# Key norms spread by TensorE, x sums in row groups, angles ahead of the products, and a statistics sum kept on chip, in a gated convolution and dilated attention block on one core

## The chip, the cores and the metric

The kernel runs on one core of one Trainium2 chip. A core has five engines that work beside each other: TensorE (PE) for products, VectorE (DVE), ScalarE (ACT) and GpSimd (POOL) for elementwise work, and SyncE (SP), which here issues the DMAs (transfers). Data lie in on-chip memory of 128 partitions (SBUF), products arrive in eight accumulator banks of 128 x 512 numbers (PSUM), and what doesn't fit goes to the memory off chip (DRAM, names that end in `_d`). Each engine works through its own queue and waits for the others by semaphores. The metric is the device time of one execution in microseconds (us).

## What is computed

One decoder layer on x of 2048 tokens by 1024 channels, all in float32:

```python
mod = silu(c) @ w_ada + b_ada
shift, scale, gate = split(mod, 3)
h = rms_norm(x, norm_w) * (1 + scale) + shift
a, b, g_conv, q, k, v, g_attn, m_conv, m_attn = split(h @ w_in, SPLIT_POINTS)

u = depthwise_causal_conv(a * sigmoid(b), conv_w, conv_b)     # 31 taps
u = silu(layer_norm(u, conv_ln_w, conv_ln_b)) * silu(g_conv)
y_conv = u @ w_conv_out

q = rope(rms_norm(q, q_norm_w), positions)                    # 12 heads of 128
k = rope(rms_norm(k, k_norm_w), positions)
# three groups of four heads; query t attends t, t-d, ..., t-window
# (window, dilation) = (128, 1), (512, 4), (2048, 16)
o = sum over groups of softmax(lse)[g] * attention(q, k, v)[g]
y_attn = (o * silu(g_attn)) @ w_attn_out

out = (sigmoid(m_conv) * y_conv + sigmoid(m_attn) * y_attn) @ w_out
x = x + gate * out
```

Three sums of this matter below: the mean square of each token of x, the mean square of each head of the keys (a "K-norm", one per token and head), and the mean over channels that `layer_norm` takes of the convolution's output.

## The kernel before, in words

The tokens are worked in two halves of 1024. The large product with `w_in` is done by a scheme with seven products instead of eight for each 2 x 2 block of quarters (A11, A12, A21, A22 of the activations, B11 to B22 of the weights, with sums such as S1 and T1), each with its numbers split in a high and a low part, so that one quarter product is twelve matmuls of 128 x 512 (lines 310 to 314). Such a group of twelve is a **product** here; there are 562. ACT makes the high parts, DVE or POOL the low ones, and POOL or ACT and DVE the sums. The first sixteen products of half 0 use plain quarters (`PLAIN`, line 304), because the sums of quarters are not there yet.

The program numbers the products (slots) and keeps an agenda: `at_slot(s, f, where)` (line 470) puts a piece of other work beside product s, at a place in it ("act", "vec", "tail", "store" and so on). PE's queue and, in most of the kernel, those of DVE, ACT, POOL and SP follow the order in which the program issues the work; an instruction that waits holds up those behind it in its engine's queue.

The stages, in order: the start (loads of x and w_ada, the squares of x, their mean, the scaling by the adaLN numbers `mod`; the rope's sines and cosines, called angles, made on DVE in two big tiles), half 0's queries, keys and values with the attention of its heads, half 0's gates and convolution, the same for half 1, the end of the convolution, then the layer norm and the output projections in blocks.

Places that the change touches:

- *K-norms* (`rotate`, lines 579 to 704, called once for each of 12 pairs of query heads and 12 of key heads; `which` is 0 for queries, 1 for keys). ACT squares the projected heads; PE sums the squares over channels into a few rows of a bank (`sums`, line 602), ACT copies these out (`rows`). For queries PE turns the rows by two transposes (`queries`, line 613), DVE adds epsilon, POOL takes the power -1/2 (`query_roots`, line 621). For keys the rows go to DRAM in four stores and come back by a load into `stk`, one token in each partition (`keys`); POOL makes the roots (`key_roots`); these go to DRAM (`rsk_d`) and come back by two loads that repeat them over 64 partitions each into `rsk` (`key_spread`); DVE multiplies both tiles of the heads by it (`key_scale`, line 644, two instructions of 128 x 1024).
- *turn_v* (line 564): values are transposed on PE into bank "t" (line 570), copied by ACT to `vev` (line 572) and stored.
- *Banks* (line 80): tags z, s and o have two banks each, t and u one each.
- *The squares of x*: `x_square` (line 881) squares one 128 x 512 tile on ACT and sums over channels on PE with the squares as the stationary operand, four products with one output column each; `x_roots` (line 888) adds epsilon and takes the root; `x_spread` (line 894) has PE spread the four columns of roots over 128 x 512; `x_scale` (line 900) multiplies. `first_part` (line 928) makes the high and low part of an A quarter, the low part on the engine that it is given.
- *later_x* (lines 1204 to 1222): half 1's tokens are loaded in rows, squared with a sum on ACT; the roots of 1024 tokens are stored to `rsx_d` and come back spread.
- *Weight sums* T1 to T4 of half 0's first columns are made on POOL (`sum_weights`) and stored for half 1.
- *The statistics sum*: `usum` is the sum over channel blocks of the convolution's output; each half's is stored to `usum_d`, and after the convolution the whole is loaded into a tile of 128 x 2048 (line 1446). PE sums it over partitions into `pm` (line 1498), from which the layer norm `d` goes on. The projections' input `ma` is loaded behind (line 1584), and DVE makes `yt` of it and the product `ya` (line 1590).

## Time and profile before

| | |
|---|---|
| median of 3 runs | 2518.55 us (2515.42 to 2518.6) |
| profiled execution, its time | 2517.68 us |
| its span in the profile | 2515.7 us |
| mean granted clock of PE | 0.965 |
| DMA | 463.39 MB, mean 184 GB/s |

A span is what lies between the first and the last instruction of the profiled execution. A row of a timeline has the start, the length, the engine, the line of the kernel, the operation, what it writes and reads, and in brackets how long the engine was idle before and for what it waited. A row of the stages gives, for a stretch of time, the busy time of PE, PE's weight loads, DVE, ACT, POOL (with the number of instructions each), the granted clock of PE, the share of the DMA engines and GB/s.

### The profile page before, as it was taken

To read this page: it belongs to the slowest core of one execution; us is meant where nothing else is said; L and a number is where in the kernel's file an instruction comes from. 1 tells how busy PE (TensorE), PEld (TensorE's weight loads), DVE (VectorE), ACT (ScalarE), POOL (GpSimd) and SP (SyncE) were. 2 spreads that over 40 slices of the span, in tenths; PEclk is the share of its full clock that TensorE was granted. 3 is DMA by queue.
4 is the path that set the end of the run, shared out by engine and by line. 5 is a ranking of instruction groups with operands and counts; after the bars stand their busy time and mean duration, and the time that the engine had idled before them with its cause. 6 is when DMAs were issued, how large, how long until landed. Compare 5 with 4: busy or idle time off the path is not lost. (4 is left out here: it accounts for less than half of the span.)

```text
span 2515.7 us, 34990 instructions
## 1 busy us (share of the span) xinstructions
PE 2347.1 (93%) x11628; PEld 1903.8 (76%) x11628; DVE 1763.4 (70%) x2889; ACT 1072.5 (43%) x2163; POOL 1100.2 (44%) x860
## 2 busy tenths in 40 slices
PE   7879789999989999989799899999999988999999
PEld 6556567777878888767688778787888866888887
DVE  5768674762699999955654454558999977877644
ACT  3643344444554444534444334553444443422311
POOL 2466444435445779825433233445656640000231
PEclk8889989999999999989999999999999998999999
DMA  7465567557654446643666555755445458876553
GB/s 257 151 167 173 150 224 217 162 185 241 203 183 159 150 151 197 209 153 108 174 178 197 173 163 181 248 170 170 158 133 155 143 187 307 290 262 200 176 160 104
DMA packets 313116, 463.39 MB, mean 184 GB/s; under 512 B 34468, under 2 KB 138212, under 8 KB 312808
## 3 DMA queue, kind: packets, MB, share of 16 engines
q1 hardware_dynamic: 298664, 435.46, 55.4%
q10 hardware_dynamic: 14272, 25.72, 2.8%
q8 instruction: 91, 1.49, 0.2%
q14 instruction: 89, 0.73, 0.1%
HBM read 293.99 MB, written 167.06 MB: 183 GB/s over the span
## 5 line engine op out<-in xcount | busy, mean ns | idle before, releaser
L247 POOL TENSOR_TENSOR slT<-wT,shT 128x512 fp32r<-128x512 f32 x192 | 259.6, 1354 | 283.7 <-ACT shT L246 253.4
L247 POOL TENSOR_TENSOR slB<-wB,shB 128x512 fp32r<-128x512 f32 x142 | 190.5, 1342 | 194.5 <-ACT shB L246 172.1
L246 ACT ACTIVATE shB<-wB 128x512 fp32r<-128x512 f32 x234 | 147.3, 630 | 201.6 <-issue 38.0
L247 POOL TENSOR_TENSOR slT<-wB,shT 128x512 fp32r<-128x512 f32 x94 | 126.8, 1353 | 174.7 <-ACT shT L246 148.9
L246 ACT ACTIVATE shT<-wT 128x512 fp32r<-128x512 f32 x198 | 124.2, 628 | 170.6 <-DMA wT<-tT_d 27.7
L372 DVE SCALAR_TENSOR_TENSOR ce<-ut,chan,ce 128x512 f32<-128x512 f32 x240 | 179.8, 749 | 3.6
L401 DVE SCALAR_TENSOR_TENSOR ce<-us,pair_taps,ce 128x512 f32<-128x512 f32 x240 | 179.8, 749 | 3.2
L385 DVE SCALAR_TENSOR_TENSOR cq<-ut,chan,cq 128x512 f32<-128x512 f32 x208 | 154.9, 745 | 0.0
L778 DVE CUSTOM_DVE_ANT_0 sm<-ps,mask,rqq 128x256 f32<-128x256 f32 (+1 forms) x192 | 78.1, 444 | 102.5 <-PE ps L766 73.8
L241 POOL TENSOR_TENSOR wB<-wB,wB 128x512 f32<-128x512 f32 x76 | 105.5, 1388 | 57.2 <-DVE slB L247 38.7
L246 ACT ACTIVATE shT<-wB 128x512 fp32r<-128x512 f32 x114 | 71.5, 628 | 83.0 <-PE paab L314 24.9
L796 DVE COPY pT<-ptp 128x512 f32<-128x512 f32 (+2 forms) x96 | 58.8, 612 | 55.2 <-PE ptp L794 54.9
L247 DVE TENSOR_TENSOR slB<-wB,shB 128x512 fp32r<-128x512 f32 x92 | 70.8, 771 | 37.8 <-ACT shB L246 19.0
L819 PE MATMUL po<-v,pT 128*128 128x128 f32 x560 | 84.8, 283 | 11.7 <-DVE pT L796 11.7
L819 PEld LDWEIGHTS po<-v,pT 128*128 128x128 f32 x560 | 77.1, 196 | 19.5 <-DVE pT L796 12.2
L137 POOL TENSOR_SCALAR stf<-stf 128x4 f32<-128x4 f32 x4 | 1.4, 340 | 200.7 <-DVE stf L1514 142.1
L766 PE MATMUL ps<-qk 128*128 128x128 f32 x512 | 79.0, 284 | 0.0
L1686 ACT ACTIVATE yh<-yq 128x512 fp32r<-128x512 f32 x48 | 27.3, 623 | 117.8 <-POOL yq L1680 46.1
L766 PEld LDWEIGHTS ps<-qk 128*128 128x128 f32 x512 | 69.8, 201 | 0.3 <-issue 0.2
L785 ACT ACTIVATE sm<-sm,osb 128x256 f32<-128x256 f32 (+1 forms) x128 | 58.3, 458 | 13.3 <-DVE osb L778 9.7
L825 ACT ACTIVATE osb<-po 128x256 f32<-128x256 f32 x64 | 24.7, 386 | 87.9 <-PE po L819 87.3
L644 DVE TENSOR_TENSOR spare_lo<-spare_lo,rsk 128x1024 f32<-128x1024 f32 x16 | 20.8, 1302 | 58.8 <-DMA rsk<-rsk_d 58.8
(798 smaller groups left out, 7832.5 us busy)
## 6 DMA issues: line engine op xcount, KB each, us to landing
wB<-in_w_in_dram SPq DMA_DIRECT2D x272, 256.0 KB
wT<-tT_d SPq DMA_DIRECT2D x160, 256.0 KB
tT_d<-wB SPq DMA_DIRECT2D x114, 256.0 KB
qk<-qk_d SPq DMA_DIRECT2D x96, 256.0 KB
v_d<-vev SPq DMA_DIRECT2D x48, 256.0 KB
qk_d<-spare_hi SPq DMA_DIRECT2D x48, 256.0 KB
qk_d<-spare_lo SPq DMA_DIRECT2D x48, 256.0 KB
v<-v_d SPq DMA_DIRECT2D x96, 128.0 KB
```

Of the source, the lines that this page charges most:

```text
L241: nc.gpsimd.tensor_tensor(dst, x0, x1, op=ALU.subtract)
L246: nc.scalar.activation(h, q[name], AF.Copy)
L247: eng.tensor_tensor(l, q[name], h.bitcast(F32), op=ALU.subtract)
L372: stt(box["e"], e[:, 1 + j : 513 + j], chan[:, cb, 2 * j : 2 * j + 1], box["e"], op0=ALU.mult, op1=ALU.add)
L385: stt(box["o"], o[:, 2 + j : 514 + j], w, psum_o, op0=ALU.mult, op1=ALU.add)
L401: stt(dst, box["both"][:, 1 + j : 513 + j], pair_taps[:, cb, j : j + 1], box["e"], op0=ALU.mult, op1=ALU.subtract if j == 0 else ALU.add)
L766: nc.tensor.matmul(ps[:, c : c + P], box["q"][i], kt, start=True, stop=True)
L778: nc.vector.tensor_tensor_reduce(sm[:, a:z], ps[:, a:z], m[:, 256 - (z - a) :], rq[:, b, u % 2 : u % 2 + 1], 3e38, ALU.add, ALU.min, box[" ...
L785: nc.scalar.activation(sm[:, a:z], sm[:, a:z], AF.Exp, scale=-1.0, bias=box["low"][i], accum_out=box["total"][i])
L796: nc.vector.tensor_copy(valid(pT), valid(pt))
L819: nc.tensor.matmul(po[:, P * i : P * i + P], box["pT"][:, c : c + P], vt, start=(m == 0), stop=(m == count[i] - 1))
L1686: nc.scalar.activation(h, src, AF.Copy)
```

## The change

**Keys.** The two transposes, DVE's epsilon (`more`) and POOL's root (`roots`) now serve queries and keys alike. For keys PE then spreads the roots: `spread(c)` is eight products with a column of roots, repeated 64 times, as the stationary operand and the identity as the moving one, which fill one bank; DVE scales two half tiles of 128 x 512 from that bank, and the second `spread` uses the same bank "t" after that. The four stores, the load, the store and the two repeating loads are gone. The squares' sums, the rows and the transposes stand one product earlier; the first spread stands two products behind the transposes, the second one more. `turn_v` uses banks t and u in turn.

**The start.** Squares of x are summed with a 32-wide block of ones as the stationary operand and the squares as the moving one, in four row groups, into 128 columns; DVE copies the rows, and PE transposes them. For the second half of the columns x's scaling takes in adaLN's scale. All low parts of these first quarters are made on DVE, all low parts of the plain weights on POOL. The order of `PLAIN` changes (ten splits instead of twelve), and the second part of w_ada is loaded ahead of B21 and B22. Of the angles' steps nine stand ahead of x's roots and eight more ahead of x's scaling, instead of six ahead and the rest beside the first products. The permuted copies of the angle tables go from ACT to POOL.

**Other places.** `later_x` moves from slots 7 to 15 to slots 21 to 38, and its roots are spread by PE (two times four products, copied by ACT) and not through `rsx_d`. The weight sums of half 0's first columns are no longer made and stored; half 1 makes them itself. Half 0's `usum` is stored and loaded back when half 1's convolution opens, into one half of the wide tile; half 1's sum is made in the other half of it, so that no store and load stand ahead of `pm`.

The core of the diff:

```diff
-            if cb == KC - 1:
-                nc.sync.dma_start(usum_d[:, HS * half : HS * half + HS], us)
+            if cb == KC - 1 and half == 0:
+                nc.sync.dma_start(usum_d, us)
...
-                pt = bank("t", f"pt{n}_{col}{c}")
+                pt = bank("tu"[i % 2], f"pt{n}_{col}{c}")
...
+        def turned():
+            pt = box["pt"] = bank("t", f"prq{n}")
             for c in range(2):
                 nc.tensor.transpose(pt[:, P * c : P * c + P], box["rows"][:, c], ident)
-            st = box["st"] = rb["p"].tile([P, 48], F32, tag="st", name=f"st{n}", bufs=1)
-            got = pt[:, : 2 * P].rearrange("p (c q m) -> p c q m", c=2, q=4)[..., :2]
+
+        def more():
+            st = box["st"] = rb["p"].tile([P, 32], F32, tag="st", name=f"st{n}", bufs=2)
+            got = box["pt"][:, : 2 * P].rearrange("p (c q m) -> p c q m", c=2, q=4)[..., :2]
             nc.vector.tensor_scalar(st[:, :16].rearrange("p (c q m) -> p c q m", c=2, q=4), got, EPS, None, op0=ALU.add)
 
-        def query_roots():
+        def roots():
             st = box["st"]
-            rq = edge.tile([P, 16], F32, tag="rq", name=f"rq{n}", bufs=4)
             nc.gpsimd.tensor_tensor(st[:, 16:32], st[:, :16], mhalf, op=ALU.pow)
-            nc.gpsimd.tensor_scalar(rq, st[:, 16:32], ISQ, None, op0=ALU.mult)
-            heads_rq[half, u0] = rq.rearrange("p (b m) -> p b m", m=2)
-
-        def keys():
-            ss = dram.tile([2, HS], F32, name=f"ss{n}_d")
-            for q in range(4):
-                nc.sync.dma_start(ss.rearrange("h (c q i) -> q h c i", c=2, q=4)[q], box["rows"][32 * q : 32 * q + 2])
-            st = box["st"] = rb["p"].tile([P, 48], F32, tag="st", name=f"st{n}", bufs=1)
-            nc.sync.dma_start(st[:, :16], ss.rearrange("h (p c) -> (h p) c", c=16))
-
-        def key_roots():
-            st = box["st"]
-            rsqrt_cols(st[:, 32:48], st[:, :16], 16, st[:, 16:32])
-
-        def key_spread():
-            rs_d = dram.tile([2, HS], F32, name=f"rs{n}_d")
-            nc.sync.dma_start(rs_d.rearrange("h (p c) -> (h p) c", c=16), box["st"][:, 32:48])
-            rs = box["rs"] = rp["p"].tile([P, HS], F32, tag="rs", name=f"rs{n}", bufs=1)
-            for h in range(2):
-                nc.sync.dma_start(rs[64 * h : 64 * h + 64], rs_d[h][None, :].to_broadcast([64, HS]))
-
-        def key_scale(i):
-            return lambda: tt(reg[i], reg[i], box["rs"], op=ALU.mult)
+            if which == 0:
+                rq = edge.tile([P, 16], F32, tag="rq", name=f"rq{n}", bufs=4)
+                nc.gpsimd.tensor_scalar(rq, st[:, 16:32], ISQ, None, op0=ALU.mult)
+                heads_rq[half, u0] = rq.rearrange("p (b m) -> p b m", m=2)
+
+        def spread(c):
+            def f():
+                rs = box["rs"] = bank("t", f"rs{n}_{c}")
+                for q in range(4):
+                    for m in range(2):
+                        a = 16 + 8 * c + 2 * q + m
+                        nc.tensor.matmul(rs[64 * m : 64 * m + 64, P * q : P * q + P], box["st"][:, a : a + 1].to_broadcast([P, 64]), ident,
+                                         start=True, stop=True, skip_group_check=True)
+            return f
+
+        def key_scale(c, i):
+            x = reg[i][:, 512 * c : 512 * c + 512]
+            return lambda: tt(x, x, box["rs"], op=ALU.mult)
...
-            start, last = e6 + 2, e6 + 4
+            start, last = e6 + 2, e6 + 3
             count = (3, 3, 3, 3) if which else (3, 3, 2, 2, 2)
         else:
-            sq = ((e4 + 1, 0, 0), (e5, 1, 1), (e5 + 1, 0, 1), (e6 + 1, 1, 0))
-            start, last = e5 + 2, e6 + 3
-            count = (3, 3, 2, 2, 2) if which else (2,) * 6
+            sq = ((e4, 0, 0), (e4 + 1, 1, 1), (e6, 0, 1), (e6 + 1, 1, 0))
+            start, last = e6, e6 + 2
+            count = (2,) * 6
         for s, c, i in sq:
-            at_slot(s, square(c, i), "act2")
-            at_slot(s + 1, sums(c, i), "tail")
+            at_slot(s, square(c, i), "act" if s > e6 else "act2")
+            at_slot(max(s, e6 - 2), sums(c, i), "tail")
...
-        at_slot(last, rows, "act2")
+        at_slot(last, rows, "act")
+        at_slot(last, turned, "tail")
+        at_slot(last + 1, more)
+        at_slot(last + 1, roots)
         if which == 0:
-            at_slot(last + 1, queries, "tail")
-            at_slot(last + 2, query_roots)
             for i in range(2):
                 at_slot(end, store(i), "load")
         else:
-            at_slot(last, keys, "store")
-            at_slot(last + 1, key_roots)
-            at_slot(last + 2, key_spread, "store")
-            s = last + 3
-            assert s >= end
+            for c in range(2):
+                at_slot(last + 2 + c, spread(c), "tail")
+                for i in range(2):
+                    at_slot(last + 3 + c, key_scale(c, i))
+            assert last + 3 + 1 >= end - 1
             for i in range(2):
-                at_slot(s + i, key_scale(i))
-                at_slot(s + i + 1, store(i), "load")
-            kept_by[half, u0] = s + 2
+                at_slot(last + 5, store(i), "load")
...
+    def x_sum(k, t, pm):
+        sq = squares.pop((k, t))
         for b in range(4):
-            nc.tensor.matmul(pm[:, b : b + 1], sq[:, P * b : P * b + P], ones[:, :1],
-                             start=(k == 0 and b == 0), stop=(k == KC - 1), skip_group_check=True)
-
-    def x_roots(t, pm):
-        st = su.tile([P, 12], F32, tag="xst", name=f"xst{t}", bufs=2)
-        nc.vector.tensor_scalar(st[:, 8:12], pm[:, :4], EPS, None, op0=ALU.add)
+            nc.tensor.matmul(pm[32 * b : 32 * b + 32, :P], ones[:, :32], sq[:, P * b : P * b + P],
+                             start=(k == 0), stop=(k == KC - 1), skip_group_check=True)
+
+    def x_rows(t, pm):
+        rows = su.tile([P, 512], F32, tag="sq", name=f"xrow{t}", bufs=5)[:, :P]
...
+    def x_roots(t, pm, rows):
+        nc.tensor.transpose(pm[:, P : 2 * P], rows, ident)
...
+    angle_steps(9)
     pm = bank("t", "xm0")
     for k in range(KC):
-        x_square(k, 0, pm)
-    pr = x_spread(0, x_roots(0, pm))
-    for k in range(KC):
-        x_scale(k, 0, pr)
+        x_square(k, 0)
+        x_sum(k, 0, pm)
+    st = x_roots(0, pm, x_rows(0, pm))
+    angle_steps(8)
...
+    def later_spread(c):
+        pr = bank("o", f"rsx{c}")
+        for b in range(4):
+            a = 24 + 4 * c + b
+            nc.tensor.matmul(pr[:, P * b : P * b + P], xst1[:, a : a + 1].to_broadcast([P, P]), ident, start=True, stop=True)
+        nc.scalar.activation(xh["rs"][:, 512 * c : 512 * c + 512], pr, AF.Copy)
...
+        if half:
+            sums_of["p"] = ctx.enter_context(pool("sum"))
+            wide = sums_of["u"] = sums_of["p"].tile([P, S], F32, tag="wide", name="usum")
+            nc.sync.dma_start(wide[:, :HS], usum_d)
         p = opened(cv, pool("cv"))
-        cv["usum"] = p.tile([P, HS], F32, name=f"usum{half}")
+        cv["usum"] = wide[:, HS:] if half else p.tile([P, HS], F32, name="usum0")
...
-    sp = ctx.enter_context(pool("sum"))
-    usum = sp.tile([P, S], F32, tag="wide", name="usum")
-    nc.sync.dma_start(usum, usum_d)
+    sp, usum = sums_of["p"], sums_of["u"]
```

How the order moves on the engines, at three places. First, DVE at the second key pair of half 1. `spare_lo` holds the keys that are scaled, `rsk` the roots, `sm` and `osb` the scores of a head's attention, `pT` a transposed attention tile. Before:

```order
L778 ISA sm_1_3_11211,osb_1_3_11210<-ps_1_3_11205,mask,rqq_0_10486 128x256
L778 ISA osb_1_3_11210 128x1
L778 ISA sm_1_3_11211,osb_1_3_11210<-ps_1_3_11205,mask,rqq_0_10486 128x256
L778 ISA osb_1_3_11210 128x1
L644 TENSOR_TENSOR spare_lo<-spare_lo,rsk_1_11200 128x1024
L512 TENSOR_TENSOR spare_hi<-spare_hi,pcq_2_11089 128x32x16
L796 COPY pT_1_2_11237<-ptp_1_2_11232 128x512
L644 TENSOR_TENSOR spare_lo<-spare_lo,rsk_1_11200 128x1024
```

After:

```order
L657 TENSOR_TENSOR spare_lo<-spare_lo 128x512
L658 TENSOR_TENSOR spare_lo<-tmk_1_10_11144,tmk_1_11_11146 128x512
L635 TENSOR_TENSOR spare_lo<-spare_lo,rsk_1_0_11205 128x512 x2
L768 ISA sm_1_3_11283,osb_1_3_11282<-ps_1_3_11277,mask,rqq_0_10494 128x256
L768 ISA osb_1_3_11282 128x1
L768 ISA sm_1_3_11283,osb_1_3_11282<-ps_1_3_11277,mask,rqq_0_10494 128x256
L768 ISA osb_1_3_11282 128x1
L635 TENSOR_TENSOR spare_lo<-spare_lo,rsk_1_1_11256 128x512 x2
L507 TENSOR_TENSOR spare_hi<-spare_hi,pcq_2_11155 128x32x16
L786 COPY pT_1_2_11310<-ptp_1_2_11305 128x512
```

The scaling of the first columns now stands ahead of the scores and that of the second columns behind them, where the first scaling of 128 x 1024 stood; no scaling stands behind the copy `pT` any more. On PE, the two spreads of this pair stand at the end of one product and of the next (`paq` and `pak` are the banks of products, `ptp` an attention tile's transposes); the first of them with its surroundings:

```order
L309 MATMUL paq_2_10962<-S_hi_9810,shT_1_4096_11069 128x512
L309 MATMUL paq_2_10962<-S_lo_9811,shT_1_4096_11069 128x512
L309 MATMUL paq_2_10962<-S_hi_9810,slT_1_4096_11070 128x512
L629 MATMUL rsk_1_0_11205<-ident,stk_1_11148 64x128 x8
L784 MATMUL ptp_1_1_11214<-ident,sm_1_1_11101 128x128 x4
L309 MATMUL pak_2_11241<-A_hi_9526,shB_1_5632_11106 128x512
L309 MATMUL pak_2_11241<-A_lo_9527,shB_1_5632_11106 128x512
L309 MATMUL pak_2_11241<-A_hi_9526,slB_1_5632_11107 128x512
```

There was nothing between `paq` and `ptp` before; what is behind the spread in this queue goes on only when the roots `stk` are there.

Second, DVE at the start. `spare_lo` and `spare_hi` are the angles, `xm` the sums of squares, `xst` the four columns for the roots, `xr` their spread, `hf` the tiles of x. Before:

```order
L944 TENSOR_SCALAR spare_lo<-spare_lo 128x1024
L890 TENSOR_SCALAR xst_307<-xm_258 128x4
L901 TENSOR_TENSOR hf_0_171<-hf_0_171,xr_310 128x512
L901 TENSOR_TENSOR hf_0_172<-hf_0_172,xr_310 128x512
L901 TENSOR_TENSOR hf_0_173<-hf_0_173,xr_310 128x512
```

After:

```order
L952 TENSOR_TENSOR spare_hi<-spare_hi,spare_lo 128x1024
L955 SCALAR_TENSOR_TENSOR spare_hi<-spare_lo,spare_hi 128x1024
L955 SCALAR_TENSOR_TENSOR spare_hi<-spare_hi 128x1024
L885 COPY xrow_309<-xm_260 128x128
L891 TENSOR_SCALAR xst_312<-xm_260 128x4
L955 SCALAR_TENSOR_TENSOR spare_hi<-spare_lo,spare_hi 128x1024
L955 SCALAR_TENSOR_TENSOR spare_hi<-spare_hi 128x1024
L955 SCALAR_TENSOR_TENSOR spare_hi<-spare_lo,spare_hi 128x1024
L955 SCALAR_TENSOR_TENSOR spare_hi<-spare_hi 128x1024
L955 SCALAR_TENSOR_TENSOR spare_hi<-spare_lo,spare_hi 128x1024
L955 SCALAR_TENSOR_TENSOR spare_hi<-spare_hi 128x1024
L956 TENSOR_SCALAR spare_hi<-spare_hi 128x1024
```

Ten more rows of 128 x 1024, all but the last two steps of the angles, stand ahead of the first `hf` row, which follows these.

Third, SP at the end of the convolution. `d` is the layer norm's input, `gg` a gate, `fraw` the raw input of a projection. Before:

```order
L414 DMA usum_d<-usum_14737 128x1024
L1492 DMA d_18897<-u_d 128x2x512
L1492 DMA d_19127<-u_d 128x2x512 x4
L1529 DMA gg_0_19404<-g_d 128x512
L1529 DMA gg_1_19433<-g_d 128x512
L1529 DMA gg_2_19484<-g_d 128x512
L1446 DMA usum<-usum_d 128x2048
L1584 DMA ma_0_18888<-ma_d 128x512
L1070 DMA fraw<-ag_d 128x512
```

After:

```order
L1534 DMA d_19015<-u_d 128x2x512 x3
L1534 DMA d_19245<-u_d 128x2x512 x4
L1626 DMA ma_0_19006<-ma_d 128x512
L1077 DMA fraw<-ag_d 128x512
L1626 DMA ma_1_19035<-ma_d 128x512
L1077 DMA fraw<-ag_d 128x512
```

The sum's store and load are gone, `gg` stands behind the first `ma` and `fraw` rows, and `ma` follows the `d` rows.

227 lines of the change are left out of this document (127 added, 100 removed), and 6 rows, old and new, of the table PLAIN.

## The prediction

> **What bounds the kernel now.** I read the head of the page first, then the stages with the busy time of each engine, then the list of what TensorE (PE) waits for.
>
> ```profile
> span 2515.7 us, 34990 instructions
> PE 2347.1 (93%) x11628; PEld 1903.8 (76%) x11628; DVE 1763.4 (70%) x2889; ACT 1072.5 (43%) x2163; POOL 1100.2 (44%) x860
> ```
>
> PE is the bound: it is idle for 2515.7 - 2347.1 = 168.6 us. What a change can bring here is that idle time, the time PE runs at a lower granted clock, and small products that are done more cheaply; what it adds to PE is paid nearly in full. The stages (columns: length, busy time of PE, PEld, DVE, ACT, POOL with instruction counts, granted clock, DMA share, GB/s) show where the idle time lies:
>
> ```profile
> 30.20:120.00 89.80, 78.20 (x350) 57.90 (x351) 62.25 (x72) 52.74 (x83) 34.68 (x20) 0.79 0.48 158
> 120.00:187.80 67.80, 51.16 (x245) 38.22 (x243) 45.40 (x42) 33.77 (x63) 48.26 (x33) 0.87 0.67 171
> 187.80:557.50 369.70, 333.05 (x1787) 260.96 (x1782) 247.64 (x361) 159.54 (x325) 177.83 (x120) 0.94 0.60 186
> 557.50:1040.00 482.50, 468.06 (x2272) 390.60 (x2272) 405.17 (x768) 228.35 (x511) 309.88 (x263) 0.99 0.56 183
> 1040.00:1140.00 100.00, 84.16 (x354) 66.84 (x353) 63.95 (x83) 48.86 (x82) 41.23 (x30) 0.91 0.55 177
> 1140.00:1604.00 464.00, 428.15 (x2527) 348.73 (x2525) 246.80 (x453) 200.66 (x450) 174.47 (x127) 0.97 0.57 169
> 2063.00:2095.00 32.00, 14.49 (x52) 10.81 (x51) 11.16 (x18) 4.46 (x8) 0.00 (x0) 0.68 0.91 322
> 2095.00:2516.00 421.00, 417.12 (x1821) 336.32 (x1819) 281.74 (x433) 122.68 (x205) 50.01 (x40) 1.00 0.65 208
> ```
>
> The rows in order are the start, the run-up to the first keys, the queries and keys of half 0, its gates, the turn to half 1, the queries and keys of half 1, the end of the convolution, and the projections. The change touches all but the gates and the projections. Its named targets are the longest waits (total, times, longest):
>
> ```profile
> PE po L819 <- DVE pT L796: 40.0, 9, 10.5
> PE ptv L570 <- ACT vev L572: 18.0, 9, 6.0
> PE pm L1498 <- DMA usum<-usum_d: 17.5, 1, 17.5
>   DMA rsk<-rsk_d: 91.7, 12
> POOL stk L137 <- DMA stk<-ssk_d: 80.3, 12, 12.7
> ```
>
> The last two are the waits on the key roots' way through memory: DVE stands 91.7 us before the 12 key scalings, POOL 80.3 us before the roots. How that reaches PE shows in the second key pair of half 1:
>
> ```profile
> 1253.76 1.23 DVE L644 TENSOR_TENSOR spare_lo<-spare_lo,rsk 128x1024 f32<-128x1024 f32 x1 [12.69 <-DMA rsk<-rsk_d]
> 1255.86 0.70 DVE L796 COPY pT<-ptp 128x512 f32<-128x512 f32 x1
> 1256.61 0.80 PE L819 MATMUL po<-pkv,pT 128*128 128x128 f32 x2 [10.48 <-DVE pT L796]
> 1249.80:1256.60 6.80, 0.00 (x0) 0.00 (x0) 2.84 (x4) 0.00 (x0) 0.00 (x0) 0.50 0.55 153
> 1256.60:1260.10 3.50, 3.49 (x17) 3.49 (x17) 1.09 (x1) 1.38 (x4) 0.40 (x1) 0.50 0.92 233
> ```
>
> The copy of an attention tile is queued behind the key scaling on DVE; PE stands 10.48 us for it, and then works 3.5 us more at half clock, which costs 1.75 us. [...]
>
> **The keys (K-norms).** Removed for each of 12 pairs: four stores, a load, the roots' store and two broadcast loads, and with them both waits. PE idles 369.7 - 333.05 = 36.7 us in half 0 and 464 - 428.15 = 35.9 us in half 1; the missing clock is at most 0.06 x 369.7 + 0.03 x 464 = 36 us. Not all of it is the keys' (part comes from DVE being behind with sums), so I take three quarters of the idle time, 54 us, and of the clock, which partly falls on idle time, 20 us: 74 us go.
>
> Added on PE for each pair: two transposes of the rows (queries have theirs already) and two spreads of eight products, each with a 64-wide stationary column and 128 moving columns. No row has that shape; the nearest:
>
> ```profile
> 62.14 1.05 PE L897 MATMUL xr<-ident,xst 128*128 128x128 f32 x8
> 206.09 0.43 PE L602 MATMUL pssq<-sqq,sel 128*32 128x128 f32 x8
> 107.78 0.60 PE L570 MATMUL ptv<-ident,spare_hi 128*128 128x128 f32 x4
> ```
>
> Four full-width products (eight records) take 1.05 us, four 32-wide ones beside each other 0.43. So a spread of eight lies between 2 x 0.43 = 0.86 and 2 x 1.05 = 2.1 us; 64-wide lies between the two, and I take 1.3. With two transposes (0.30) a pair costs 2.9 us, 12 of them 35 us; the ends are 24 and 54. [...]
>
> New waits: PE has the spread in its own queue, two products (slots) behind the transposes, and it waits there for the root on POOL. The queries of before run the same way, from the transposes to the root:
>
> ```profile
> 367.07 0.38 PE L613 MATMUL prqq<-ident,ssrq 128*128 128x128 f32 x2
> 373.43 3.27 POOL L621 TENSOR_TENSOR stq<-stq,mhalf 128x16 f32<-128x16 f32 x1 [6.26 <-DVE stq L616]
> 1163.65 0.38 PE L613 MATMUL prqq<-ident,ssrq 128*128 128x128 f32 x2
> 1166.23 3.35 POOL L621 TENSOR_TENSOR stq<-stq,mhalf 128x16 f32<-128x16 f32 x1 [3.28 <-DVE stq L616]
> 1820.45 2.72 PE pcg_ma_d L314 x12
> ```
>
> The second instance is done 5.9 us after the transposes began, the first, where DVE was behind, 9.6 us. Two products are at least 2 x 2.72 = 5.4 us, and with the small work beside them 6 to 7. So usually little waits; behind the spread stand all later products, and DVE waits for them. The second spread also needs the bank that DVE reads in two scalings first. I take 0.5 us a pair, 6 us (ends 0 and 48, which is the late query's 4 us each time). The squares' sums also move a slot earlier on PE; ACT has half its time free there (159.54 of 369.7), so I cost that at nothing; if ACT is late, it is in the 48. The scaling itself becomes four PSUM reads of half the width; L901 and L644 give it below:
>
> ```profile
> L901 DVE TENSOR_TENSOR hf<-hf,xr x16: 676/679/689, 23.6 to 75.3; 128x512 f32<-128x512 f32 x16
> L644 DVE TENSOR_TENSOR spare_lo<-spare_lo,rsk x16: 1210/1224/1915, 211.6 to 1509.6; 128x1024 f32<-128x1024 f32 x16
> ```
>
> 4 x 0.68 against 2 x 1.22 is 0.3 us more, beside PE work on a DVE with a third of its time free. The other x-norm of half 1 (rsx) adds eight full products, 2.1 us. Keys in all: -74 + 35 + 6 + 2 = -31 us. The ends: -83 with all the idle time and clock gone and spreads at 24 (-72.6 - 36 + 24 + 2), +30 with spreads at 54 and waits at 48.
>
> **120 to 188 us.** The store of the other norm in four-byte pieces (rsx_d, at 140.4) goes, as do eight stores of weight sums, and the loads of x with their 16 squares move to later slots.
>
> ```profile
> 142.00:152.00 10.00, 6.15 (x28) 4.76 (x26) 0.00 (x0) 0.00 (x0) 5.97 (x5) 0.94 1.11 40
> 153.45 0.60 ACT L572 ACTIVATE vev<-ptv 128x512 f32<-128x512 f32 x1 [12.69 <-DMA v_d<-vev]
> 157.17 0.79 PE L314 MATMUL pcq<-S_hi,shB 128*128 128x512 f32 x1 [9.02 <-DVE spare_hi L512]
> ```
>
> For ten microseconds the DMA engines are fully busy and move only 40 GB/s; ACT waits 12.69 us for a buffer that is being stored, and PE 9.02 us for the eviction behind it. Without that store this gap has no cause left. PE idles 16.6 us here and lacks at most 0.13 x 67.8 = 8.8 us of clock; I take 15 and 4, less 2 for DVE, which gets six subtractions from POOL: -17 us (ends -25 and -8; the second if only the 9.02 go).
>
> **The start.** The sixteen first products need 16 x 2.72 = 43.5 us and take the 89.8 us of their stage. In it the sums of squares stand alone on PE for 11.3 us:
>
> ```profile
> 45.80 11.32 PE L885 MATMUL xm<-ones,xsq 128*128 128x1 f32 x64
> 33.21 6.58 POOL L935 TENSOR_TENSOR A_lo<-hf,A_hi 128x512 fp32r<-128x512 f32 x2 [11.85 <-DVE hf L934]
> 38.69 2.17 DVE L948 SCALAR_TENSOR_TENSOR spare_hi<-spare_lo,spare_hi 128x1024 f32<-128x1024 f32 x1
> ```
>
> Eight groups at 0.43 make that 3.4 us, and a transpose 0.15: -7.5. The low parts of the first products, 3.3 us each on POOL beside DVE's angles (2.17 us), go to DVE (0.69). Against that, all but two of the angle steps now stand ahead of the scaling of x on DVE: some 6 us (six of 1.2 us, less what overlaps), so the first product starts near 36 us, not 30.2. Then 43.5 plus 3.4, plus about 5 for the two adaLN products and transposes, plus some 14 for waits and the half clock (30 before) is 66: the end moves from 120 to 102, -18 us (ends -30 and +6). POOL copies of the tables are in no row; between 1.3 and 6.6 us each by the POOL row above. I take 2.5, hidden unless they hold up the fourth low part behind them.
>
> **The statistics sum.** Its store and load go; DVE's last addition stays. PE's 17.5 us and about 2.7 us of half clock are the most there is. But the projections' own inputs then end last:
>
> ```profile
> 2075.66 0.32 SPq L1584 DMA_DIRECT2D ma<-ma_d  x1
> ```
>
> ```profile
> 2084.21 2.04 PE L1498 MATMUL pm<-usum,ones 128*128 128x512 f32 x2 [17.51 <-DMA usum<-usum_d]
> ```
>
> ```profile
> 2084.84 0.69 DVE L1590 SCALAR_TENSOR_TENSOR yt<-ma,ya 128x512 f32<-128x512 f32 x1 [20.05 <-DMA ma<-ma_d]
> ```
>
> `ma` lands 2084.84 - 2075.66 = 9.2 us after its issue, half a microsecond behind the sum. In the changed order it stands right behind the `d` loads, so it is issued some 6 us earlier (the sum's store and load and the three `gg` are off ahead of it) and lands near 2079. Until its first result is stored, PE can fill the six banks of these products, 2.72 us each; two and a half are still to come where PE stops now, 7 us of work, and the sum's two records another 2. So a wait of 5 to 6 us for `ma` takes the place of the 17.5: 12 gained, with 2 of clock -14 us (ends -20, all of it, and -4, if `ma` lands no sooner than it does).
>
> **The turn to half 1.** The four weight sums of half 0 were kept; now they are made again in half 1:
>
> ```profile
> L241 POOL TENSOR_TENSOR wB<-wB,wB 128x512 f32<-128x512 f32 x76 | 105.5, 1388 | 57.2 <-DVE slB L247 38.7
> ```
>
> Eight of these, 11 us, on a POOL that is busy 41.23 of the stage's 100: mostly hidden. In return the loads of the kept sums go. I take +2 (ends -3 and +6).
>
> **Sum.** -31 - 17 - 18 - 14 + 2 = -78 us. The profiled execution took 2517.7 (its span of 2515.7 and 2.0 around it), 0.9 below the median of the runs. 2517.7 - 78 = 2439.7: I predict **2440**.
>
> **Rivals.** *The root's wait moves into PE's queue.* The spread is placed two products after the transposes; should it stand for each pair the 4 us by which the late query exceeds 5.4, the keys cost 42 us more: 2482. For it: 9.6 us in the instance where DVE was behind. Against: 5.9 in the other. Chance 0.12.
>
> *Start and transition give nothing.* With the angles ahead of the scaling the first product starts 6 us later and DVE, which now makes every low part, becomes the bound of the stage; and `ma`'s landing holds PE as the sum did. Then start 0, transition -4: 2440 + 18 + 10 = 2468. For it: DVE is busy 62.25 of 89.8 us there. Against: the POOL's 11.85 us wait for the scaled x shows that low parts, not angles, ended last. Chance 0.08.
>
> *Slower: the spread stalls the whole queue.* One mechanism: PE waits at the first spread for POOL's root (4 us), at the second for the bank that DVE must read twice first (2 x 0.68 us, behind attention copies some 3.2), and works at half clock after (1.5): 8.7 us a pair, 8.2 more than taken, 12 x 8.2 = 98: 2538. It decides from 78 / 12 + 0.5 = 7 us a pair. For it: DVE is the engine already behind (10.48 us at `pT`). Against: its 91.7 us of waiting for memory, which made it late, is gone. Chance 0.05; a part of it, which just eats the gain, 0.02.
>
> *Better: the gaps vanish altogether.* The keys at their -83, 52 below what is taken: 2388. For it: PE's longest wait is for DVE's copies (40.0 us), and DVE's is for `rsk` (91.7). Against: DVE stays busy with the same sums. Chance 0.05. That the change doesn't do what it says can hardly be: no store or load of key norms is left in its order.
>
> **How the numbers follow.** The forecast has 0.68. The chances sum to 0.68 + 0.12 + 0.08 + 0.05 + 0.05 + 0.02 = 1. The terms hang little together, so that their ends don't fall on one side at once; the range 2395 to 2490 takes in the forecast and the first two rivals (0.88, less some tails of the keys' term) and leaves out the better case and the slower ones. 0.2%, 5 us, is about what a measurement of this kernel can tell from no change. Faster by more: 0.93; within: 0.02; slower: 0.05.
>
> **What would show it.** Keys: no wait on rsk_d or stk; PE's wait at `rs` for POOL's `st` under 1 us a pair, a spread at 1.3 us (0.86 to 2.1), idle time of the stages of half 0 and 1 down to about 10 us each. 120 to 188: no stretch of full DMA at 40 GB/s, the 9.02 us gap gone. Start: first product near 36 us, sixteenth's end near 102. Transition: PE's largest gap 5 to 6 us, for `ya`'s bank, DVE waiting for `ma`. Turn: length 100 us within 6. I am wrong if PE's waits at the spreads exceed 7 us a pair, if DVE is full (over 90%) from the start to the first keys, or if PE's clock stays lower than in before.

## The result, and the profile after

The changed kernel takes 2427.57 us (median of 4 runs, 2426.46 to 2431.16), the kernel before beside it 2518.57: a ratio of 0.964 (95% interval 0.9624 to 0.9657). That is 91 us less where 78 were forecast; the forecast time was 2440, its range 2395 to 2490.

The head of the page of the profiled execution after:

```profile
span 2424.7 us, 35722 instructions
PE 2321.6 (96%) x12054; PEld 1884.0 (78%) x12054; DVE 1764.5 (73%) x2926; ACT 1071.8 (44%) x2159; POOL 1090.0 (45%) x844
```

PE is busy 25.5 us less than before and idle 103.1 us in place of 168.6. The stages after, cut at the same work as those of before as nearly as it goes (columns as there):

```profile
0.00:35.00 35.00, 13.01 (x140) 6.12 (x140) 24.11 (x34) 12.04 (x18) 7.06 (x22) 0.96 0.98 342
35.00:105.70 70.70, 63.32 (x351) 46.18 (x352) 46.68 (x59) 35.75 (x58) 26.45 (x17) 0.85 0.39 134
105.70:151.60 45.90, 45.90 (x249) 35.72 (x247) 39.20 (x40) 30.79 (x59) 31.03 (x20) 1.00 0.62 189
151.60:500.90 349.30, 327.55 (x1941) 259.81 (x1944) 236.01 (x377) 167.59 (x342) 173.69 (x114) 0.99 0.62 196
...
1085.00:1530.00 445.00, 434.11 (x2744) 354.90 (x2743) 263.87 (x479) 206.67 (x457) 174.90 (x122) 1.00 0.57 170
...
1980.00:2005.00 25.00, 20.55 (x78) 16.13 (x77) 19.06 (x28) 7.52 (x12) 0.00 (x0) 0.86 0.86 313
```

From the sixteenth product's end to the first pair's keys PE has no idle time at all (45.90 of 45.90), and in half 1's queries and keys 10.9 us (445.00 - 434.11) at full clock, where it had 35.9 at 0.97. In half 0's queries and keys 21.8 us are left (349.30 - 327.55), where the prediction's signs had about 10.

To see where the 91 us come from, the same products are looked up in both timelines. PE's records of each bank are as many before as after (576 for `paq`, 576 for `pak`), so that the n-th is the same product:

| place in PE's queue | before, us | after, us | ahead by | gained in the stretch | forecast |
|---|---|---|---|---|---|
| end of the sixteenth product | 119.8 | 105.5 | 14.3 | 14.3 (start) | 18 |
| end of the first pair's last `pak` | 187.6 | 151.6 | 35.9 | 21.6 (120 to 188) | 17 |
| end of half 0's last `pak` | 549.9 | 500.9 | 49.0 | 13.1 (keys of half 0) | 31 with half 1's |
| first `paag` of half 0's gates | 929.7 | 875.8 | 54.0 | 5.0 (gates of half 0) | none |
| end of half 1's first pair of keys | 1172.8 | 1116.1 | 56.8 | 2.8 (turn) | -2 |
| end of half 1's last `pak` | 1563.5 | 1485.3 | 78.2 | 21.4 (keys of half 1) | as above |
| end of the last `pag_g_d` | 2059.4 | 1980.2 | 79.3 | 1.1 (gates of half 1) | none |
| end of the last `ya` | 2171.7 | 2080.6 | 91.1 | 11.8 (sum) | 14 |

The keys with the gates behind them give about 40 us (13.1 + 5.0 + 21.4; half 0's attention goes on into its gates). So every term is within 9 us of its forecast. The experiments ask whether they are so for the reasons given.

What PE waits for after (total, times, longest):

```profile
PE rsk L629 <- POOL stk L617: 13.1, 6, 4.2
PE pcv L309 <- DVE spare_hi L507: 9.1, 1, 9.1
...
PE rsk L629 <- DVE spare_lo L635: 6.4, 4, 2.1
...
PE ya L1518 <- DVE yt L1632: 4.6, 2, 4.4
...
PE rsk L629 <- DVE spare_hi L635: 3.1, 2, 1.7
```

The waits for `pT` (40.0 us before) and for `usum` (17.5) are gone. The spreads wait 13.1 us for POOL's root and 6.4 + 3.1 = 9.5 for DVE's scalings: 22.6 us, 1.9 a pair. The longest single wait left, 9.1 us at `pcv`, stands in the turn to half 1, where the kernel before waited too (6.2).

### The profile page after: what moved, and what is told of

It reads as the page before. It is cut to its first block, busy times and chain, and to the rows that moved or that the text cites. A ratio compares the mean times of both kernels' runs of the same rounds, so it can differ in the third digit from the quotient of the medians.

```text
span 2424.7 us, 35722 instructions
## 1 busy us (share of the span) xinstructions
PE 2321.6 (96%) x12054; PEld 1884.0 (78%) x12054; DVE 1764.5 (73%) x2926; ACT 1071.8 (44%) x2159; POOL 1090.0 (45%) x844
## 4 chain that ended last, share of the span: by engine, by line
PE 72%; DVE 9%; DMA 3%; issue 2%; POOL 1%; ACT 1%; SPq 0%; DVEq 0%; ACTq 0%; POOLq 0%
PE yc L1518 7%; PE paab L309 6%; PE oa L1800 4%; PE pak L309 3%; PE paq L309 3%; PE pag_ma_d L309 3%; PE pcab L309 3%; PE pav L309 3%; PE pag_mc_d L309 3%; PE po L809 3%; PE ya L1518 3%; PE ps L756 3%; PE pag_g_d L309 2%; PE pck L309 2%; PE pcq L309 2%
## 5 line engine op out<-in xcount | busy, mean ns | idle before, releaser
L247 POOL TENSOR_TENSOR slT<-wT,shT 128x512 fp32r<-128x512 f32 x188 | 254.1, 1352 | 314.0 <-ACT shT L246 266.7
L241 POOL TENSOR_TENSOR wB<-wB,wB 128x512 f32<-128x512 f32 x80 | 112.5, 1407 | 47.8 <-DVE slB L247 35.8
L617 POOL TENSOR_TENSOR stk<-stk,mhalf 128x16 f32<-128x16 f32 x12 | 38.4, 3203 | 49.6 <-DVE stk L613 37.9
```

What stands on the lines that cost most here:

```text
L241: nc.gpsimd.tensor_tensor(dst, x0, x1, op=ALU.subtract)
L247: eng.tensor_tensor(l, q[name], h.bitcast(F32), op=ALU.subtract)
```

## The experiments

Times are medians. Ratios are to runs of the kernel before that were taken beside them on the same chip (medians 2518 to 2521 us), with their 95% interval; the change itself has 0.964 (0.9624 to 0.9657). A line of three dots in an edit or a view stands for what is left out.

### The way of the key roots, and their products

`keys_memory`: the key roots through memory again, at the changed products.

```diff
...
-            for c in range(2):
-                at_slot(last + 2 + c, spread(c), "tail")
...
+            at_slot(last, keys, "store")
+            at_slot(last + 1, key_roots)
+            at_slot(last + 2, key_spread, "store")
...
```

> The changed kernel with the key roots sent through memory again, at the changed slots (one product earlier than in the kernel before). Theory: the waits for memory were what the keys' part gained, about 40 us of the 91 (the two stretches of queries and keys and the gates of half 0 behind them became 19 and 21 us shorter). So 2427.6 + 40 = 2468 us (2455 to 2480), DVE's wait for rsk back at 80 us or more in all, PE's for pT at 30 or more. Rival: starting the sums a product earlier and the two banks of turn_v did it; then at most 2440 us, with PE waiting little for pT though DVE waits for rsk.

Measured: 2429.62 us, ratio 0.9646 (0.9633 to 0.966), the same as the change. The rival holds: without the spreads by PE nothing is lost. PE is busy 2304.1 us, 17.5 less than with the spreads, and idle as much more.

`keys_before`: the same, and squares, sums, rope and rows (of queries and keys alike) at the products of before too.

```diff
-            sq = ((e4, 0, 0), (e4 + 1, 1, 1), (e6, 0, 1), (e6 + 1, 1, 0))
-            start, last = e6, e6 + 2
-            count = (2,) * 6
+            sq = ((e4 + 1, 0, 0), (e5, 1, 1), (e5 + 1, 0, 1), (e6 + 1, 1, 0))
+            start, last = e5 + 2, e6 + 3
+            count = (3, 3, 2, 2, 2) if which else (2,) * 6
...
```

> The changed kernel with the whole of rotate as before: key roots through memory, and squares, sums, rope and rows at the kernel before's products. With the roots through memory at the changed products the time was 2429.6 us, so what gained some 40 us in the queries and keys is not the way of the roots. Theory E: it is the earlier start (sums and rows one product earlier, rope from the sixth product on), which leaves memory its time; then 2455 to 2470 us here, DVE's waits for rsk back from 42.8 to 80 us or more and PE's for pT from 14.3 to 30 or more. Rival L: it is other work that was taken out of the way (the later x work, the banks of turn_v); then at most 2440 us.

Measured: 2473.93 us, ratio 0.9804 (0.9775 to 0.9833): 44 us slower than with the same trip at the changed products. The waits in `keys_before`:

```profile
DVE spare_lo L642 <- DMA rsk<-rsk_d: 71.5, 8, 13.5
DVE spare_hi L642 <- DMA rsk<-rsk_d: 28.1, 4, 14.4
PE po L817 <- DVE pT L794: 35.5, 7, 10.3
```

and in `keys_memory`:

```profile
DVE spare_lo L642 <- DMA rsk<-rsk_d: 28.4, 8, 6.9
DVE spare_hi L642 <- DMA rsk<-rsk_d: 14.4, 3, 6.3
PE po L816 <- DVE pT L793: 14.3, 7, 5.4
```

One product earlier takes DVE's wait from 71.5 + 28.1 = 99.6 to 28.4 + 14.4 = 42.8 us and PE's from 35.5 to 14.3. Theory E holds in its waits; the time is 4 us above its range.

`earlier_only`: that move alone, in the kernel before (the edit above the other way round, with the roots through memory).

> The kernel before with one part alone: the squares, sums, rope and rows at the changed products, the roots still through memory, turn_v in one bank, the later x work as before. Theory E: 2518.1 - 30 = 2488 us (2478 to 2498). Rival L: 2505 us or more.

Measured: 2489.29 us, ratio 0.9871 (0.984 to 0.9902). Theory E holds here too, with 32 us against the runs beside it. The move has a price here: PE waits 21.8 us for ACT's squares of the queries, 5.1 in the kernel before:

```profile
PE pssq L602 <- ACT sqq L589: 21.8, 7, 7.9
```

`spread_late`: the spreads by PE, with squares, sums, rope and rows at the products of before. Unlike in the change, the second spread is in bank u here. The keys that this kernel stores in three of the six pairs of each half are not those that it should: their stores, in this order, are issued only when the tiles have been given to other heads. No instruction is left out, but a wait could be, so that the time is good to a few us.

```diff
-                rs = box["rs"] = bank("t", f"rs{n}_{c}")
+                rs = box["rs"] = bank("tu"[c], f"rs{n}_{c}")
...
-            start, last = e6, e6 + 2
+            start, last = e5 + 2, e6 + 3
...
-                at_slot(last + 5, store(i), "load")
+                at_slot(last + 4, store(i), "store")
```

> The changed kernel with the squares, sums, rope and rows of rotate at the kernel before's products, and the key roots spread by PE (the second spread in bank u, the stores a place earlier, since the order needs it). With the roots through memory these products gave 2473.9 us, the changed ones 2429.6. Theory: the two parts replace each other, because each alone makes the roots come before DVE needs them; then 2430 to 2442 us here, with no wait of PE for pT above 3 us. Rival: the earlier products count for themselves (DVE's and ACT's order), whichever way the roots go; then 2460 us or more.

Measured: 2431.54 us, ratio 0.9651 (0.963 to 0.9672), and no wait for `pT` above 3 us. The theory holds: the two parts replace each other.

| key roots | products of before | changed products |
|---|---|---|
| through memory | 2473.9 | 2429.6 |
| spread by PE | 2431.5 (bank u) | 2427.6 |

With its second spread in bank t the 2431.5 would be some 6 us more, by the sum under `three_moves` below; that changes nothing in the reading.

How the earlier products hide the trip is seen in the second key pair of half 1. DVE in `keys_memory`, from the rope's last rows (L664, L665) to the scaling (L642):

```profile
1180.86 1.56 DVE L664 TENSOR_TENSOR spare_lo<-spare_lo 128x512 f32<-128x512 f32 x1
1182.45 0.69 DVE L665 TENSOR_TENSOR spare_lo<-tmk,tmk 128x512 f32<-128x512 f32 x1
1184.45 1.23 DVE L642 TENSOR_TENSOR spare_lo<-spare_lo,rsk 128x1024 f32<-128x1024 f32 x1 [1.31 <-DMA rsk<-rsk_d]
```

ACT's copy of the rows (`ssrk`) starts at 1168.11 in this kernel and at 1229.25 in the kernel before, and the scaling 16.3 us behind it here and 24.5 there (the median of the 12 pairs is 18.7 and 19.4). The trip is hardly shorter. But the rope ends at 1183.1 here, 15 us behind the copy; in the kernel before at 1239.3, 10 us behind it:

```profile
1238.66 0.69 DVE L667 TENSOR_TENSOR spare_lo<-tmk,tmk 128x512 f32<-128x512 f32 x1
```

The last of a head's scores on DVE behind it (L778) end at 1241.07. After that DVE has nothing ahead of the scaling and waits the 12.69 us that the prediction shows. The copy now stands one product further ahead of the rope's end, and most of the trip lies beside the rope.

### The spreads' waits

`epsilon_first`: DVE adds epsilon ahead of the rope's rows of that product.

```diff
+        at_slot(last + 1, more)
+        at_slot(last + 1, roots)
         ops = rope()
...
-        at_slot(last + 1, more)
-        at_slot(last + 1, roots)
```

> The changed kernel with one order turned: in the product behind the transposes DVE adds epsilon (and POOL takes the root) ahead of the rope's steps, not behind them. Theory: PE's 13.1 us at the spreads for POOL's root come from DVE, which reaches the epsilon late; they fall under 4 us, and 2427.6 - 9 = 2419 us (2415 to 2423). Rival: PE then waits for DVE's scalings in the place of the root, 9.5 us now, as DVE's work is the same; then 2425 to 2430 us.

Measured: 2420.84 us, ratio 0.9605 (0.9587 to 0.9624), 6.7 us less than the change; the interval meets that of the change at its edge. In its profile:

```profile
PE rsk L629 <- DVE spare_lo L635: 7.9, 5, 2.1
...
PE rsk L629 <- POOL stk L617: 5.6, 3, 2.2
...
PE rsk L629 <- DVE spare_hi L635: 2.9, 3, 1.7
```

The wait for the root falls from 13.1 to 5.6 us, not under 4, and that for the scalings rises from 9.5 to 10.8. So the theory holds for the most part, its time too, but the gain is hardly clear of the noise.

### The stage from 120 to 188 us

`rsx_tensor`: the kernel before with the other half's x roots spread by PE.

```diff
-        nc.sync.dma_start(rsx_d.rearrange("(j p) -> p j", p=P), xst1[:, 24:32])
...
-        nc.sync.dma_start(xh["rs"], rsx_d[None, :].to_broadcast([P, HS]))
+        for c in range(2):
+            at_slot(LATER_0 + 1, lambda c=c: later_spread(c), "tail")
```

> The kernel before with one part alone: the other half's x roots are spread by TensorE (eight products, two copies) and not stored in four-byte pieces and loaded back. Theory: that store fills the DMA queues in the stretch from the first queries to the first keys' end, which the change made 21.6 us shorter; the 9.02 us wait of PE at pcq and ACT's 12.7 us for vev go, and the whole takes 2518.6 - 14 = 2504 us (2498 to 2509). Rival: the loads and squares of x and the stores of weight sums in the same slots crowd that stretch; then 2513 us or more, and ACT still waits for v_d longer than 5 us.

Measured: 2507.08 us, ratio 0.9958 (0.9938 to 0.9979). The median is in the theory's range, though the five runs lie far apart (2499.9 to 2514.25 us). In the trace PE's wait at `pcq` is gone and ACT's longest wait for `v_d` is 2.9 us. The first pair's last `pak` ends at 180.1, 7.5 us earlier than in the kernel before, though the stage starts 1.5 us later, so 9.0 gained in it, what PE's wait was. The change gained 21.6 there.

`later_early`: the change with the loads, squares and sums of the later x work early again.

```diff
-LATER_X, LATER_ROOM, LATER_BUSY = 21, 2, 1
+LATER_X, LATER_ROOM, LATER_BUSY = 7, 2, 1
...
-        at_slot(LATER_X + 2 * j, lambda j=j: later_x(j), "load")
+        at_slot(LATER_X + j, lambda j=j: later_x(j), "load")
...
```

> The changed kernel with the later x work early again: loads and squares at products 7 to 15, root at 17, scaling and sums from 22 on; roots still spread by PE. Theory L: its loads, squares and DVE's sums held the first queries and keys; 2427.6 + 10 to 20 = 2438 to 2448 us, lost between the sixteenth product and the second key pair. Rival: once the four-byte store is gone there is room for it there; then 2425 to 2432 us.

Measured: 2425.12 us, ratio 0.9619 (0.9592 to 0.9646): no difference from the change. In the trace the first pair's last `pak` ends 5.3 us later than after, though the stage starts 2.5 us earlier; by half 0's fourth pair it is 13.8 behind. But there it is ahead with the attention, whose first scores (`ps`) PE makes at 296.3 us and after at 334.2; it ends half 0's scores earlier too (665.1 and 707.2), and at half 1's start it is 4.4 us ahead. So 7.8 of the 21.6 us were moved, not won.

`turn_one_bank`: the change with `turn_v` in bank t alone.

```diff
-                pt = bank("tu"[i % 2], f"pt{n}_{col}{c}")
+                pt = bank("t", f"pt{n}_{col}{c}")
```

> The changed kernel with turn_v in bank t alone, as before. PE waited 18.0 us for vev before at these transposes, and waits under 3 us now. Theory: the second bank takes these waits away; 2427.6 + 12 = 2440 us (2436 to 2443). Rival: they came from stores that were late (the four-byte store, 12.7 us once) and are gone with those; then 2426 to 2432 us.

Measured: 2434.46 us, ratio 0.9653 (0.9631 to 0.9676), between the two; its interval overlaps that of the change. PE waits 4.8 us for `vev` here, none after, and 18.0 before, so most of that wait does not come back with the single bank. Nor was it the four-byte store's: `rsx_tensor` is without that store and waits 19.4. What took it away stays open.

```profile
PE ptv L565 <- ACT vev L567: 4.8, 5, 2.0
```

```profile
PE ptv L570 <- ACT vev L572: 19.4, 9, 6.2
```

The first line is of `turn_one_bank`, the second of `rsx_tensor`.

### The start

`x_columns`: the change with x's squares summed as before.

```diff
-                nc.tensor.matmul(pm[32 * b : 32 * b + 32, :P], ones[:, :32], sq[:, P * b : P * b + P],
+                nc.tensor.matmul(pm[:, b : b + 1], sq[:, P * b : P * b + P], ones[:, :1],
...
```

> The changed kernel with x's squares summed as before: the squares stationary, one column of ones moving. Theory: PE is held by these products beside the first sixteen; the sums of the two halves of x's columns cost 25.3 us of PE before and 8.8 now, half of it in the stage of the first products: 2427.6 + 7.5 = 2435 us (2432 to 2439). Rival: the squares on ACT and the landing of x end last in both places; then 2426 to 2430 us.

Measured: 2443.81 us, ratio 0.9704 (0.9687 to 0.9721), 16.2 us above the change and more than the theory had. Its runs lie far apart (2437.8 to 2448.7 us), and the profiled one is the fastest: in it the sixteenth product ends at 116.8 us, 11.3 later than after, and the end comes 11.4 later. The sums' busy time over both halves of x's columns (columns here: length, PE, PEld, DVE, clock, DMA share, GB/s), in this kernel:

```profile
0.00:2435.00 2435.00, 25.30 (x128) 25.50 (x128) 0.32 (x2) 0.99 0.58 185
```

and after:

```profile
0.00:2424.00 2424.00, 8.82 (x130) 3.98 (x130) 0.90 (x4) 0.99 0.58 186
```

Of the 16.5 us between them 11.3 reach the sixteenth product in this execution. 2.8 of these are there at the first product already (37.8 us for 35.0): the sums of x's first columns, beside the landing of x, count in part too.

`angles_beside`: the change with the angles' steps beside the first products, as before.

```diff
-    angle_steps(9)
+    angle_steps(6)
...
-    angle_steps(8)
...
+    at_slot(0, lambda: angle_steps(10))
...
```

> The changed kernel with the angle steps of DVE as before: six ahead of x's roots, ten beside the first product, three more two products on, and the permuted tables made a product later. The first product starts at 35.0 us with the angles ahead and at 30.2 before. Theory: the 4.8 us are paid back in the sixteen first products, where DVE makes all low parts; their end comes 3 to 10 us later than 105.5, and the whole takes 2431 to 2437 us. Rival: the angles ahead only cost, since DVE has room beside the first products (46.7 of 70.7 us busy); then the end comes at 101 to 104 us, and the whole takes 2420 to 2426 us.

Measured: 2431.93 us (2425.58 to 2434.58), ratio 0.9646 (0.9633 to 0.9659): no difference from the change that is clear of the noise. In the profiled execution, the fastest of the five, the first product starts 6.6 us earlier and the sixteenth ends 0.7 us earlier. The median lies in the theory's range, but neither theory's end of the sixteenth product came: what the angles ahead cost at the first product they give back by the sixteenth, and no more.

### The statistics sum

`sum_memory`: the change with the whole sum loaded after the convolution.

```diff
...
-    sp, usum = sums_of["p"], sums_of["u"]
+    sp = ctx.enter_context(pool("sum"))
+    usum = sp.tile([P, S], F32, tag="wide", name="usum")
+    nc.sync.dma_start(usum, usum_d)
```

> The changed kernel with the statistics sum stored and loaded whole after the convolution. Theory: the transition gained 11.9 us (from 79.2 to 91.1 ahead) by this alone; so 2439.5 us (2437 to 2443), and PE's longest wait there is again 15 us or more, for usum. Rival: the projections' own input, which waits for the same loads, ends last anyway; then 2428 to 2432 us.

Measured: 2439.8 us, ratio 0.9692 (0.9679 to 0.9706), 12.2 above the change. The theory holds, and the wait is back:

```profile
PE pm L1538 <- DMA usum<-usum_d: 17.3, 1, 17.3
```

### A faster version

`three_moves`: `later_early`, `epsilon_first`, and the second spread in bank u.

```diff
...
-                rs = box["rs"] = bank("t", f"rs{n}_{c}")
+                rs = box["rs"] = bank("tu"[c], f"rs{n}_{c}")
...
```

> The changed kernel with the later x work early (2425.1 us alone), the epsilon ahead of the rope, and the second spread in bank u, so that it doesn't wait for the scalings of the first. Theory: PE's 22.6 us of waits at the spreads go for the most part: 2425.1 - 9 - 8 = 2408 us (2403 to 2416). Rival: bank u is held then where the next pair's sums need it, and the waits only change their name; then 2420 us or more.

Measured: 2412.8 us, ratio 0.9574 (0.9555 to 0.9593): faster than both kernels, some 15 us under the change, in the theory's range. PE's waits at the spreads are 9.3 us for the root and none of any length for the scalings; 3.2 come up in their place at `pssq`, the next pair's sums in bank u, which the rival named, but which is the smaller part:

```profile
PE rsk L629 <- POOL stk L617: 9.3, 3, 4.4
...
PE pssq L597 <- DVE spare_lo L635: 3.2, 2, 1.7
```

The two other moves alone had 2.5 and 6.7 us, 2418.4 together. If they add, bank u is worth the rest, some 6 us; no run has it by itself.

## Why the prediction was right, and where its reasons were not

**The keys.** The size was near (31 forecast, some 40 measured); a step of it failed. "Removed for each of 12 pairs ... and with them both waits", with 74 us for it, took the way through memory for the cause. In the kernel before the waits were for memory, as the rows said. But the change has two parts that each end them: the way of the roots, and the squares, sums, rope and rows placed one product earlier. The prediction costed the second "at nothing" and asked only whether it might do harm. The table of four shows that alone it is worth 44 us, that PE's spreads alone are worth about as much (42, with the second in bank u), and that together they are worth 46: the second to be added brings little. In the kernel before, without the other parts of the change, the move alone was worth 32. The size held although the step failed, because either part by itself ends most of the idle time that the 74 us were read from. The 46 are more than the stretches' 40, probably since these carry the later x work that was moved into them. The spreads' own cost was well bounded: 27.32 us of PE for 24 of them, 1.14 each (1.3 taken, ends 0.86 and 2.1), and 4.55 for the transposes, so 32 for 35 forecast. Eight products with a 64-wide stationary side, at 1.14 us, stand between the 0.86 and the 2.1 of twice four with 32 and with 128. A spread and the product behind it:

```profile
1128.66 1.09 PE L629 MATMUL rsk<-ident,stk 128*64 128x128 f32 x16 [0.24 <-POOL stk L617]
1129.69 0.50 PE L309 MATMUL pak<-A_hi,shB 128*128 128x512 f32 x1
1130.02 0.39 PE L309 MATMUL pak<-A_lo,shB 128*128 128x512 f32 x1
```

The product behind the spread starts its second matmul 0.33 us after its first, where 0.23 is usual inside a product; behind groups of 128-wide products (`ptp`) it is 0.31 too, so these rows show no price of the narrower shape beyond the spread's own time.

The new waits were mis-sized: 1.9 us a pair where 0.5 was taken, inside the ends of 0 and 4. The rival "the root's wait moves into PE's queue" had the right mechanism, with 13.1 us in place of its 48; the other 9.5 are the wait for the second spread's bank, which the slower rival named. Most of the first comes from DVE's queue, which reaches the epsilon late, as `epsilon_first` shows (13.1 to 5.6 us).

**120 to 188 us.** 17 forecast, 21.6 measured. The four-byte store was 9.0 of it, as the 9.02 us gap had it; another 7.8 were the later x work, which the prediction did not price and which is paid back later. The rest, some 5 us, no run takes apart.

**The start.** 18 forecast, 14.3 measured. The first product did start near 36 us (35.0). The row-group sums gave 11.3, not 7.5, because the first half's sums count in part. The angles cost their 6 us at the first product (6.6) and give them back in the stage. The term that was mis-sized is what lies between the first product and the sixteenth's end: 66 us forecast, 70.5 measured. The sums and the transpose there take 3.1 us of PE, near the 3.4 taken, and the adaLN products with their transposes 4.0 for "about 5". But the spread of the roots and the value transposes, 3.6 us more, stand there too and were not counted. That leaves 70.5 - 43.5 - 3.1 - 4.0 - 3.6 = 16 for waits and lower clock (0.85 in the mean of this stage), where 14 were taken. The new order of `PLAIN`, the earlier load of w_ada and the low parts on DVE were not tried by themselves.

**The statistics sum.** 14 forecast, 11.8 measured. `sum_memory` shows the cause, with 12.2 us. The next wait is the one named, `ya` for `yt`, at 4.4 us where 5 to 6 was said:

```profile
1999.58 0.80 PE L1518 MATMUL ya<-ai0hi,wah 128*128 128x512 f32 x1 [4.45 <-DVE yt L1632]
```

**The turn to half 1.** +2 forecast, -2.8 measured: by that stretch alone making the weight sums again on POOL costs PE nothing that shows; no run has that part by itself.

**The slower rival** did not come: 1.9 us a pair is far from its 7.

## What to carry to other kernels

A wait names what came last, not the only way to end it. When a change both replaces a slow transfer and moves its start, price the move by itself first: here one product of head start, without any new work on TensorE, was worth as much as taking the transfer away (44 and 42 us), and the two did not add (46 together). Where a new step stands in the queue of the busiest engine, put what it waits for first in the queue of the engine that makes it: in `epsilon_first` that took TensorE's wait for the root from 13.1 to 5.6 us.

## What the runs showed of the hardware that was not expected

VectorE's rope rows took a median of 1.78 us while GpSimd added or subtracted 128 x 512 tiles, and 0.74 while it was idle. DVE and then POOL in the changed kernel, around the longest wait of a spread:

```profile
205.38 1.81 DVE L655 SCALAR_TENSOR_TENSOR spare_lo<-spare_lo,hw,sin 128x512 f32<-128x512 f32 x1
207.11 1.78 DVE L656 SCALAR_TENSOR_TENSOR spare_lo<-spare_lo,hw,cos 128x512 f32<-128x512 f32 x1
...
215.84 0.16 DVE L613 TENSOR_SCALAR stk<-prqk 128x16 f32<-128x16 f32 x1
...
216.52 0.74 DVE L655 SCALAR_TENSOR_TENSOR spare_lo<-spare_lo,hw,sin 128x512 f32<-128x512 f32 x1
```

```profile
206.60 1.74 POOL L241 TENSOR_TENSOR wB<-wB,wT 128x512 f32<-128x512 f32 x1
208.31 1.74 POOL L247 TENSOR_TENSOR slB<-wB,shB 128x512 fp32r<-128x512 f32 x1
...
216.08 3.31 POOL L617 TENSOR_TENSOR stk<-stk,mhalf 128x16 f32<-128x16 f32 x1 [2.64 <-DVE stk L613]
```

The same row of L655 took 1.81 us beside POOL's work and 0.74 when POOL made the small root. Over the whole trace of the changed kernel the median of such rows (L651, L655, L656) is 0.74 us with POOL idle (108 rows), 1.78 at least nine tenths beside its 128 x 512 work (15 rows) and 0.75 wholly beside the root (24 rows). The transposes ended at 209.8 and DVE came to the epsilon at 215.84, behind such rows; the spread then waited 4.15 us. So a busy POOL alone does not lengthen them: beside the tiles they took 2.4 times as long, but the row at 216.52 took 0.74 us beside the root, which runs for 3.31 us from 216.08. What makes the difference no run shows.

The granted clock is lower behind that wait too (columns as in the stages):

```profile
215.30:219.44 4.14, 0.00 (x1) 0.00 (x1) 4.14 (x7) 1.48 (x2) 3.36 (x2) 1.00 0.79 239
219.44:223.00 3.56, 3.56 (x20) 2.93 (x21) 3.37 (x5) 0.00 (x0) 1.18 (x1) 0.52 0.85 188
...
1134.70:1137.70 3.00, 2.99 (x38) 2.41 (x39) 1.28 (x2) 0.00 (x0) 0.50 (x1) 1.00 0.02 5
```

After 4.15 us without work PE ran 3.6 us at about half clock; after a wait of 2.00 us (ahead of 1134.70) it kept the full one. But the clock was lower behind other short waits: in the changed kernel one of 1.84 us (ahead of 249.15) was followed, a microsecond on, by 3.4 us at 0.52, in the kernel before one of 3.20 us by 3.4 us at 0.54:

```profile
249.15 0.50 PE L309 MATMUL pck<-S_hi,shB 128*128 128x512 f32 x1 [1.84 <-DVE spare_lo L507]
250.20:253.60 3.40, 3.40 (x10) 2.62 (x9) 3.31 (x6) 0.34 (x1) 3.23 (x3) 0.52 0.20 77
```

```profile
260.23 0.80 PE L314 MATMUL paq<-A_hi,slT 128*128 128x512 f32 x1 [3.20 <-POOL slT L247]
260.23:263.63 3.40, 3.40 (x9) 2.68 (x10) 0.00 (x0) 0.00 (x0) 2.41 (x2) 0.54 0.26 63
```

So the length of a wait alone does not decide in these traces; what does, they do not show.
